# Attention probabilities turned on VectorE and through device memory instead of on TensorE

## The chip, the cores and the metric

The kernel runs on one core of a Trainium2 chip. The metric is the device time of one execution in microseconds (us). A core has TensorE (PE, matrix products into PSUM banks), VectorE (DVE), ScalarE (ACT), GpSimd (POOL) and SyncE (SP). SyncE and GpSimd here mostly start transfers (DMAs), which 16 DMA engines carry out. Each engine runs its own instructions in program order and waits on semaphores for the others.

## The reference, cut to what matters

One decoder layer on 512 tokens of width 2048, in float32: a norm, an attention mixer with 16 heads of width 128 in 4 groups (4 heads share keys and values), an output projection with a residual, a norm, a SwiGLU feed-forward block of width 5632, a residual, and a last norm. With 512 tokens the "selected" branch selects every block and the window covers every token, so a head has three causal branches:

```python
q, kc, vc, ks, vs, kw, vw, gl = jnp.split(h @ w_in, bounds, axis=-1)
gates = jax.nn.sigmoid(gl)                       # three gates for each head and token
kcc, vcc = compress(kc, ...), compress(vc, ...)  # 31 compressed keys and values
p_c = masked_softmax(q @ kcc.T + bias_c, mask_c);  o_c = p_c @ vcc
p_s = masked_softmax(q @ ks.T + bias, causal);     o_s = p_s @ vs
p_w = masked_softmax(q @ kw.T + bias, causal);     o_w = p_w @ vw
out = (g0 * o_c + g1 * o_s + g2 * o_w) @ w_out
```

(This is a summary of the reference's functions in its own names.)

## The kernel before, in words

Every matrix operand is split into a high and a low part (type float32r), and each product is three TensorE products: high x high, high x low, low x high (`three`, lines 265 to 267). A split is a ScalarE copy that rounds to the high part, and a VectorE subtraction that leaves the low part (`split_from`, lines 290 and 291; for weights lines 95 and 96).

The order on every engine is written out by hand: instructions run on each engine in the order in which the program issues them. Weights come as a list of granules of up to 128 x 1024 elements. `granules` writes the list; `Weights.load` issues a granule's DMA on SyncE into one of 3 raw buffers; `Weights.split` splits it into one of 4 converted buffers; `take` hands out the next one and keeps splits and loads some granules ahead.

The attention stage stands between 205 and 722 us of the profile. It mixes two streams. One is attention, head after head. The other is `dense()`, a generator of projection products: queries for a pair of heads (`qpair`), keys and values of the next group (`kpair`, `vpair`), and at the end a part of the output projection (`partial`). `pump(h, step)` runs the dense stream forward until its count of work has reached a goal that grows by one twelfth of a head's share with each step. `drain_to(n)` runs it until n units are done. So TensorE gets dense work between the small attention pieces, and other engines get time for theirs.

A head's queries are cut into four tiles of 128 tokens. Tile t sees the keys of tiles 0 to t, 128(t+1) of them, in each of two full branches, and 31 compressed keys.

- `scores(h, t)`: TensorE writes the scores of all three branches into the PSUM tile `s` (three banks, one copy). For each branch VectorE adds the bias from `TB[h]` (or `biasc`), writes the negated sum into `P[t]` (or `CX[t]` for the compressed branch) and takes its minimum (line 773); ScalarE takes the exponential in place and its sum (line 775).
- `finish(h, t)`: VectorE inverts the sums, multiplies by the gates (lines 780 and 781), and multiplies the three branches by these factors (line 787). The compressed branch is written three times side by side, which makes 96 columns.
- `turn(h, b, kt)`: values need the probabilities with keys on partitions. For key tile kt of branch b, TensorE transposes one 128 x 128 block for each query tile t from kt to 3 into the PSUM tile `pt` (line 797, two buffers). ScalarE and VectorE split it into `pth` and `ptl` (lines 290 and 291; 799 and 800 for the compressed branch).
- `values(h, b, kt)`: TensorE adds the product with the values to the PSUM tile `o` (one bank, one copy).
- `head_out(h)`: `o` is split, and stored to device memory in `d_o` for the first 12 heads (line 824), or kept for the last 4.

The nine pieces (b, kt) of a head are turned one after another, key tile 3 first, and the values of a piece follow two pieces after its turn. The scores of tiles 3 and 2 of the next head stand in the last two steps of a head, those of tiles 1 and 0 at the start of their own head. `load_bias(h + 1)` loads the next head's bias rows into the one buffer `TB` at the start of a head (line 747).

SyncE issues the weight loads (line 79), the bias rows and the stores of `d_o`. GpSimd issues nothing between the stage's first bias row at 197 us and 803 us.

Of the kernel before, what the change touches and what calls it, by code (L numbers as in the profile page):

```python
# [10 lines left out]
F32 = mybir.dt.float32  # L11
# [27 lines left out]
TP_GAP, HN_GAP = 40, 48  # L39
RESYNC = 14  # L40
SPREAD, N_WARM = UL, 24


# [128 lines left out]
def nsa_block(ctx: ExitStack, tc: tile.TileContext, x, rel_bias, mix_g, ffn_g, fin_g, w_in, w_out,  # L172
              pos_k, w1k, w2k, pos_v, w1v, w2v, f_in, f_out, onehot, out):
    nc = tc.nc
# [131 lines left out]
    vcc = keep.tile([96, G, 128], F32R, name="vcc")  # L306
    KK, VV, Q = {}, {}, {}

    def kv_tiles(p, i):
        KK[i] = tuple(p.tile([128, 32 + 2 * S], F32R, name=f"k{i}{n}") for n in "hl")  # L310
        VV[i] = tuple(p.tile([128, NT, 256], F32R, name=f"v{i}{n}") for n in "hl")

    kv_tiles(keep, 0)

# [313 lines left out]
    with ExitStack() as st2:  # L628
        ap_ = st2.enter_context(tc.tile_pool(name="ap", bufs=2))
        ps2 = st2.enter_context(tc.tile_pool(name="ps2", bufs=2, space=PSUM))  # L630
        kv_tiles(ap_, 1)
        P = [ap_.tile([128, 96 + 256 * (t + 1)], F32, name=f"p{t}", bufs=1) for t in range(NT)]
        CX = [ap_.tile([128, 32], F32, name=f"cx{t}", bufs=1) for t in range(NT)]
        for t in range(NT):
            pool.memset(P[t][:, :96], 0.0)
        done = {"n": 0, "ns": 0}

        def stage_tile():
# [95 lines left out]
        def drain_to(n):  # L734
            while done["n"] < n:
# [2 lines left out]
                    return  # L738
                done["ns"] += c or 0

        TB, HS = {}, {}
        sc = ps2.tile([128, 3, 512], F32, name="s", bufs=1).rearrange("p a c -> p (a c)")

# [6 lines left out]
        def offs(t):  # L750
            n = 128 * (t + 1)
            return n, (96, 96 + n)

        def scores(h, t):
            g, (n, off) = h // HPG, offs(t)
# [11 lines left out]
            regions = [(CX[t][:, :NCMP], sc[:, at:at + NCMP], biasc[:, h, 24 - 8 * t:24 - 8 * t + NCMP])]  # L767
            bt = TB[h][:, S - n:].rearrange("p (n s) -> p n s", s=128)
            sw = sc[:, at + 32:at + 32 + 2 * n].rearrange("p (n b s) -> p b n s", b=2, s=128)
            for b in range(2):  # L770
                regions.append((P[t][:, off[b]:off[b] + n].rearrange("p (n s) -> p n s", s=128), sw[:, b], bt))
            for i, (p, ps, bias) in enumerate(regions):
                dve.tensor_tensor_reduce(out=p, in0=ps, in1=bias, op0=OP.add, op1=OP.min, scale=-1.0,
                                         scalar=1e38, accum_out=s["mx"][:, t, i:i + 1])
                act(p, p, AF.Exp, bias=s["mx"][:, t, i:i + 1], scale=-1.0, accum_out=s["sm"][:, t, i:i + 1])
            s[t] = [p for p, _, _ in regions]

        def finish(h, t):
            r = HS[h]["sm"][:, t]
# [2 lines left out]
            for i, p in enumerate(HS[h].pop(t)):  # L782
                o = p
                if not i:
                    o = P[t][:, :96].rearrange("p (n c) -> p n c", n=3)[:, :, :NCMP]
                    p = p.unsqueeze(1).to_broadcast([128, 3, NCMP])
                dve.tensor_scalar(o, p, r[:, i:i + 1], None, op0=OP.mult)

        def turn(h, b, kt):
            pt = ps2.tile([128, 512], F32, name="pt")  # L790
            n = S - 128 * kt
            th = ap_.tile([128, 512], F32R, name="pth")
            tl = ap_.tile([128, 512], F32R, name="ptl")
            rows = slice(0, 128) if b >= 0 else slice(0, 96)
            for t in range(kt, NT):
                src = P[t][:, :96] if b < 0 else P[t][:, offs(t)[1][b] + 128 * kt:][:, :128]
                nc.tensor.transpose(pt[rows, 128 * (t - kt):128 * (t - kt + 1)], src, ident)  # L797
            if b < 0:
                act(th[rows], pt[rows], AF.Copy)
                dve.tensor_tensor(th[32:64], pt[32:64], th[32:64].bitcast(F32), op=OP.subtract)  # L800
            else:
                split_from(pt[:, :n], th[:, :n], tl[:, :n])
            HS[h]["t", b, kt] = th[rows, :n], tl[rows, :n]

        def values(h, b, kt):
            s, g = HS[h], h // HPG
# [20 lines left out]
            del HS[h]  # L827

        load_bias(0)
        pump(-1, 9.7)  # L830
        scores(0, 3)
        pump(-1, 10.5)
        scores(0, 2)
        finish(0, 3)
        pump(-1, 11.2)
        for h in range(H):
            scores(h, 1)
            finish(h, 2)
            pump(h, 0)
            turn(h, 0, 3)  # L840
            scores(h, 0)
            finish(h, 1)
            load_bias(h + 1)
            pump(h, 1)
            turn(h, 1, 3)
            finish(h, 0)
            pump(h, 2)
            seq = [(b, kt) for kt in (3, 2, 1, 0) for b in (0, 1)] + [(-1, 0)]
            for i in range(2, 9):
                turn(h, *seq[i])  # L850
                values(h, *seq[i - 2])
                pump(h, i + 1)
            if h < 13:
                drain_to(h + 1)
            for i in range(2):
# [599 lines left out]
```

## Time and profile before

| what | before |
|---|---|
| median of 3 runs (lowest, highest) | 2156.56 us (2156.32, 2158.26) |
| the profiled execution's own time | 2156.0 us |
| its span | 2154.3 us |
| granted TensorE clock, mean | 0.999 |
| TensorE, VectorE, ScalarE, GpSimd busy | 99%, 73%, 43%, 2% |
| DMA packets, bytes | 242664, 344.02 MB |

The span is the time from the first to the last instruction in the profile. "Busy" is the share of the span in which an engine executes; for TensorE the instructions overlap in a pipeline, so what one costs is read from the distance of starts, or from the chain. The chain is the list of what had to end for the next to begin, followed back from the last instruction. A row of a group gives the line, engine and operation, what is written from what, the shape and count; then the total busy us and the mean ns of one, and after the second bar the idle time before them and what ended it. A row of waits says who waited for whom, and the total us, how often, and the longest.

### The profile page before, as it was taken

To read this page: it belongs to the slowest core of one execution; us is meant where nothing else is said; L and a number is where in the kernel's file an instruction comes from. 1 tells how busy PE (TensorE), PEld (TensorE's weight loads), DVE (VectorE), ACT (ScalarE), POOL (GpSimd) and SP (SyncE) were. 2 spreads that over 40 slices of the span, in tenths; PEclk is the share of its full clock that TensorE was granted. 3 is DMA by queue.
4 is the path that set the end of the run, shared out by engine and by line. 5 is a ranking of instruction groups with operands and counts; after the bars stand their busy time and mean duration, and the time that the engine had idled before them with its cause. 6 is when DMAs were issued, how large, how long until landed. Compare 5 with 4: busy or idle time off the path is not lost.

```text
span 2154.3 us, 37083 instructions
## 1 busy us (share of the span) xinstructions
PE 2137.4 (99%) x15081; PEld 1984.3 (92%) x15081; DVE 1580.8 (73%) x2616; ACT 928.1 (43%) x1433; POOL 53.5 (2%) x108
## 2 busy tenths in 40 slices
PE   9999999999999999999999999999999999999998
PEld 7898898988989888899999999999999888989996
DVE  5565666666665346898888888888888687878785
ACT  5344444444454224343444444343443444444354
POOL 1000000000000000000000000000000000001000
PEclk9999999999999999999999999999999999999999
DMA  7554322332352643343434433334433676878884
GB/s 230 177 153 138 91 94 80 93 96 76 98 213 96 223 139 105 111 144 121 128 118 128 128 128 117 130 117 128 137 120 126 245 283 213 292 275 307 311 328 152
DMA packets 242664, 344.02 MB, mean 160 GB/s; under 512 B 13259, under 2 KB 179195, under 8 KB 241852
## 3 DMA queue, kind: packets, MB, share of 16 engines
q1 hardware_dynamic: 228268, 272.36, 39.2%
q0 software_dynamic: 12320, 65.08, 7.8%
q10 hardware_dynamic: 1904, 4.20, 0.5%
q8 instruction: 118, 1.93, 0.4%
q14 instruction: 54, 0.44, 0.1%
HBM read 298.50 MB, written 48.34 MB: 161 GB/s over the span
## 4 chain that ended last, share of the span: by engine, by line
PE 96%; DVE 2%; ACT 1%; DMA 1%; issue 0%; SPq 0%; ACTq 0%; DVEq 0%
PE f L267 19%; PE f L266 19%; PE f L265 19%; PE proj L265 9%; PE proj L267 9%; PE proj L266 8%; PE pt L797 2%; PE pp L267 1%; PE pp L266 1%; PE pp L265 1%; PE o L266 1%; PE o L267 1%; PE s L265 1%; PE o L265 1%; PE s L267 1%; PE s L266 1%
## 5 line engine op out<-in xcount | busy, mean ns | idle before, releaser
L96 DVE TENSOR_TENSOR wlo<-raw,whi 128x1024 fp32r<-128x1024 f32 (+1 forms) x226 | 272.5, 1208 | 127.6 <-ACT whi L95 126.4
L95 ACT ACTIVATE whi<-raw 128x1024 fp32r<-128x1024 f32 (+1 forms) x226 | 234.7, 1041 | 225.8 <-DVE raw L954 122.5
L954 DVE TENSOR_TENSOR tlo<-tt,thi 128x1536 fp32r<-128x1536 f32 (+2 forms) x135 | 197.1, 1460 | 109.7 <-ACT thi L1056 88.7
L265 PE MATMUL f<-hn_h,whi 128*128 128x256 f32 x984 | 271.7, 276 | 0.8 <-ACT E L1014 0.8
L266 PE MATMUL f<-hn_l,whi 128*128 128x256 f32 x984 | 271.6, 276 | 0.0
L267 PE MATMUL f<-hn_h,wlo 128*128 128x256 f32 x984 | 271.6, 276 | 0.0
L1051 ACT ACTIVATE whi<-raw 128x1024 fp32r<-128x1024 f32 x123 | 126.0, 1057 | 292.2 <-DVE raw L954 282.0
L265 PE MATMUL proj<-hn_h,whi 128*128 128x512 f32 x512 | 204.6, 400 | 0.4 <-ACT hn_h L400 0.4
L267 PE MATMUL proj<-hn_h,wlo 128*128 128x512 f32 x512 | 200.9, 392 | 0.0
L266 PE MATMUL proj<-hn_l,whi 128*128 128x512 f32 x512 | 200.0, 391 | 0.3 <-DVE hn_l L401 0.3
L265 PEld LDWEIGHTS f<-hn_h,whi 128*128 128x128 f32 x984 | 184.7, 188 | 1.2 <-ACT E L1014 1.2
L266 PEld LDWEIGHTS f<-hn_l,whi 128*128 128x128 f32 x984 | 184.7, 188 | 0.0
L267 PEld LDWEIGHTS f<-hn_h,wlo 128*128 128x128 f32 x984 | 184.7, 188 | 0.0
L1056 ACT ACTIVATE thi<-tt 128x1536 fp32r<-128x1536 f32 x82 | 121.9, 1487 | 84.2 <-PE f L266 84.2
L954 DVE TENSOR_TENSOR wlo<-raw,whi 128x1024 fp32r<-128x1024 f32 x123 | 147.0, 1223 | 0.0
L265 PE MATMUL proj<-whi,hn_h 128*128 128x256 f32 (+2 forms) x496 | 146.4, 295 | 0.0
L267 PE MATMUL proj<-whi,hn_l 128*128 128x256 f32 (+2 forms) x496 | 145.4, 293 | 0.0
L266 PE MATMUL proj<-wlo,hn_h 128*128 128x256 f32 (+2 forms) x496 | 145.1, 293 | 0.0
L291 DVE TENSOR_TENSOR ptl<-pt,pth 128x128 fp32r<-128x128 f32 (+3 forms) x128 | 62.4, 488 | 89.4 <-ACT pth L290 89.3
L267 PE MATMUL f<-whi,tlo 128*128 128x512 f32 x320 | 124.9, 390 | 0.6 <-DVE tlo L954 0.6
L266 PE MATMUL f<-wlo,thi 128*128 128x512 f32 x320 | 125.0, 391 | 0.0
L265 PE MATMUL f<-whi,thi 128*128 128x512 f32 x320 | 124.7, 390 | 0.0
(322 smaller groups left out, 6113.1 us busy)
## 6 DMA issues: line engine op xcount, KB each, us to landing
raw<-in_ffn_w_in SPq DMA_DIRECT2D x135, 512.0 KB, 3.5
raw<-in_ffn_w_out SPq DMA_DIRECT2D x88, 512.0 KB, 5.7
raw<-in_nsa_w_in SPq DMA_DIRECT2D x48, 512.0 KB, 3.6
rawx<-in_ffn_w_in SPq DMA_DIRECT2D x41, 512.0 KB, 4.7
raw<-in_nsa_w_out SPq DMA_DIRECT2D x32, 512.0 KB, 3.8
rawx<-d_a SPq DMA_DIRECT2D x31, 512.0 KB, 5.1
raw<-in_nsa_w_in SPq DMA_DIRECT2D x56, 256.0 KB, 3.4
ah<-d_s POOLq DMA_DIRECT2D x16, 896.0 KB, 7.1
```

The source lines that it names most:

```text
L95: self.nc.scalar.activation(hi[:, :n], src, AF.Copy)
L96: self.nc.vector.tensor_tensor(lo[:, :n], src, hi[:, :n].bitcast(F32), op=OP.subtract)
L265: mm(o, ah, bh, start=start, stop=False, skip_group_check=True)
L266: mm(o, ah, bl, start=False, stop=False, skip_group_check=True)
L267: mm(o, al, bh, start=False, stop=stop, skip_group_check=True)
L291: dve.tensor_tensor(lo, psum_ap, hi.bitcast(F32), op=OP.subtract)
L797: nc.tensor.transpose(pt[rows, 128 * (t - kt):128 * (t - kt + 1)], src, ident)
L954: dve.tensor_tensor(o, a, b, op=OP.subtract)
L1051: act(h, r, AF.Copy)
L1056: act(h, ttf, AF.Copy)
```

## The change

`turn` no longer uses TensorE. After `finish` has scaled a tile's probabilities, VectorE transposes the whole tile in place in blocks of 32 x 32. For this `P[t]` is laid out as 4 x runs[t] elements a partition, with runs = 96, 160, 224 and 288: each full branch's keys are split by their 32-wide block within the key tile (index j), and the compressed branch's three copies stand in the last 32 columns of the first three j. The score reduction writes into a new tile `u` (two buffers), and the exponential reads it in the permuted order and writes `P[t]`.

After the block transpose, partition 32 i + a of the tile holds key a of a block, for the queries of block i. Four DMAs issued by GpSimd, one for each 32 partitions, write the tile to device memory as `d_p[t]` in the order (j, a, i, r); a DMA on SyncE (`fetch(t)`) reads it back into `PT` with (j, a), the key, on partitions. A piece is then a view of `PT` (`arrived`), and `turn` is just the split of that view into `pth` and `ptl`, which get three buffers each instead of two.

Tiles 0 and 2 share one buffer, as do tiles 1 and 3. The PSUM tile `pt` is gone. The second group's key and value tiles lose a spare buffer (`bufs=1`).

The order within a head becomes 12 steps. In step i below 9 piece i is turned; in steps 2 to 10 the values of piece i - 2 are multiplied. The next head's scores of tiles 3, 2, 1, 0 stand in steps 5, 7, 9, 11; its finishes of tiles 3, 2, 1 in steps 6, 8, 10, and of tile 0 in step 0 of its own head. The fetches of tiles 3 and 2 stand in steps 9 and 10, those of tiles 1 and 0 in steps 0 and 2. Because scores come half a head sooner, the dense stream makes a group's first query pair before the values instead of after, and `needed(h)` says which units must be done.

```diff
-            out += two(C_KS + c, C_KW + c)
+            out += two(C_KS + c, C_KW + c) + cols(512 * (g + 1))
             off.update((len(out) + i, 32) for i in range(4))
-            out += two(C_VS + c, C_VW + c) + cols(512 * (g + 1))
+            out += two(C_VS + c, C_VW + c)
...
-        P = [ap_.tile([128, 96 + 256 * (t + 1)], F32, name=f"p{t}", bufs=1) for t in range(NT)]
+        runs = [32 * (2 * t + 3) for t in range(NT)]
+        two = [ap_.tile([128, 4 * runs[t]], F32, name=f"p{t}", bufs=1) for t in (2, 3)]
+        P = [two[t % 2][:, :4 * runs[t]].rearrange("p (j r) -> p j r", j=4) for t in range(NT)]
...
+        PT = ap_.tile([128, 4, PT_STEP * 3 + runs[3]], F32, name="ptr", bufs=1)
+        d_p = [dram.tile([4, 32, 4, runs[t]], F32, name=f"d_p{t}") for t in range(NT)]
...
                     yield from kpair(g + 1)
+                    yield from qpair(4 * g + 4)
                     yield from vpair(g + 1)
-                    yield from qpair(4 * g + 4)
...
             for b in range(2):
-                regions.append((P[t][:, off[b]:off[b] + n].rearrange("p (n s) -> p n s", s=128), sw[:, b], bt))
-            for i, (p, ps, bias) in enumerate(regions):
-                dve.tensor_tensor_reduce(out=p, in0=ps, in1=bias, op0=OP.add, op1=OP.min, scale=-1.0,
+                u = ap_.tile([128, S], F32, name="u")[:, :n]
+                regions.append((u.rearrange("p (n s) -> p n s", s=128), u.rearrange("p (n j s) -> p j n s", j=4, s=32),
+                                branch(t, b).rearrange("p j (n s) -> p j n s", s=32), sw[:, b], bt))
+            for i, (u, v, p, ps, bias) in enumerate(regions):
+                dve.tensor_tensor_reduce(out=u, in0=ps, in1=bias, op0=OP.add, op1=OP.min, scale=-1.0,
                                          scalar=1e38, accum_out=s["mx"][:, t, i:i + 1])
-                act(p, p, AF.Exp, bias=s["mx"][:, t, i:i + 1], scale=-1.0, accum_out=s["sm"][:, t, i:i + 1])
+                act(p, v, AF.Exp, bias=s["mx"][:, t, i:i + 1], scale=-1.0, accum_out=s["sm"][:, t, i:i + 1])
...
                 dve.tensor_scalar(o, p, r[:, i:i + 1], None, op0=OP.mult)
+            dve.transpose(P[t], P[t])
+            for i in range(4):
+                pool.dma_start(d_p[t][:, :, i].rearrange("j a r -> a j r"), P[t][32 * i:32 * (i + 1)])
+
+        def fetch(t):
+
+            nc.sync.dma_start(PT[:, :, PT_STEP * t:PT_STEP * t + runs[t]], d_p[t].rearrange("j a i r -> (j a) i r"))
...
         def turn(h, b, kt):
-            pt = ps2.tile([128, 512], F32, name="pt")
...
-            for t in range(kt, NT):
-                src = P[t][:, :96] if b < 0 else P[t][:, offs(t)[1][b] + 128 * kt:][:, :128]
-                nc.tensor.transpose(pt[rows, 128 * (t - kt):128 * (t - kt + 1)], src, ident)
...
+            act(th4, src, AF.Copy)
+            if b < 0:
+                dve.tensor_tensor(th4[32:64], src[32:64], th4[32:64].bitcast(F32), op=OP.subtract)
+            else:
+                dve.tensor_tensor(tl4, src, th4.bitcast(F32), op=OP.subtract)
...
+            for i in range(STEPS):
+                if i == 0:
+                    finish(h, 0)
+                    load_bias(h + 1)
+                    fetch(1)
+                if i == 2:
+                    fetch(0)
+                if i < 9:
+                    turn(h, *seq[i])
                 if h + 1 < H:
-                    scores(h + 1, 3 - i)
-                    if i:
-                        finish(h + 1, 3)
-                values(h, *seq[7 + i])
-                if i:
-                    head_out(h)
-                pump(h, 10 + i)
+                    if i == 5:
+                        drain_to(needed(h + 1))
+                    if i in (5, 7, 9, 11):
+                        scores(h + 1, 3 - (i - 5) // 2)
+                    if i in (6, 8, 10):
+                        finish(h + 1, 3 - (i - 6) // 2)
+                    if i in (9, 10):
+                        fetch(12 - i)
+                if 2 <= i < 11:
...
+                    values(h, *seq[i - 2])
+                    if i == 10:
+                        head_out(h)
+                pump(h, i)
```

More of the change, by code (lines that the diff above doesn't have):

```diff
@@ L40 @@
 RESYNC = 14
+PT_STEP = 224
 SPREAD, N_WARM = UL, 24
@@ L307, in nsa_block, with kv_tiles @@
     KK, VV, Q = {}, {}, {}
-    def kv_tiles(p, i):
-        KK[i] = tuple(p.tile([128, 32 + 2 * S], F32R, name=f"k{i}{n}") for n in "hl")
-        VV[i] = tuple(p.tile([128, NT, 256], F32R, name=f"v{i}{n}") for n in "hl")
+    def kv_tiles(p, i, **kw):
+        KK[i] = tuple(p.tile([128, 32 + 2 * S], F32R, name=f"k{i}{n}", **kw) for n in "hl")
+        VV[i] = tuple(p.tile([128, NT, 256], F32R, name=f"v{i}{n}", **kw) for n in "hl")
     kv_tiles(keep, 0)
@@ L739, in drain_to, with needed @@
                 done["ns"] += c or 0
+        def needed(h):
+            return 4 * ((h - 2) // 4) + (1 if h % 4 > 1 else 3) if h > 1 else 0
         TB, HS = {}, {}
@@ L748, in load_bias, with branch @@
                                                  ap=[[H * UL - 1, 128], [1, S]]))
[L750 to L752 removed]
+        def branch(t, b):
+            return P[t][:, :, 32 * (t + 1) * b:32 * (t + 1) * (b + 1)]
         def scores(h, t):
[L755 removed]
+            g, n = h // HPG, 128 * (t + 1)
             (qh, ql), (kh, kl) = Q[h], KK[g % 2]
@@ L766, in scores @@
                 three(sc[:, at + c0:at + c1], qh[:, tok(t)], ql[:, tok(t)], kh[:, c0:c1], kl[:, c0:c1], True, True)
-            regions = [(CX[t][:, :NCMP], sc[:, at:at + NCMP], biasc[:, h, 24 - 8 * t:24 - 8 * t + NCMP])]
+            c = CX[t][:, :NCMP]
+            regions = [(c, c, c, sc[:, at:at + NCMP], biasc[:, h, 24 - 8 * t:24 - 8 * t + NCMP])]
             bt = TB[h][:, S - n:].rearrange("p (n s) -> p n s", s=128)
@@ L789, in turn, with arrived @@
+        def fetch(t):
+            nc.sync.dma_start(PT[:, :, PT_STEP * t:PT_STEP * t + runs[t]], d_p[t].rearrange("j a i r -> (j a) i r"))
+        def arrived(rows, c0, t0, step):
+            v = PT[:rows, :, c0:c0 + 32]
+            p, i, c = v.ap
+            return bass.AP(tensor=v.tensor, offset=v.offset, ap=[p, [step, NT - t0], i, c])
         def turn(h, b, kt):
-            pt = ps2.tile([128, 512], F32, name="pt")
             n = S - 128 * kt
-            th = ap_.tile([128, 512], F32R, name="pth")
@@ L793, in turn @@
-            tl = ap_.tile([128, 512], F32R, name="ptl")
-            rows = slice(0, 128) if b >= 0 else slice(0, 96)
-            for t in range(kt, NT):
-                src = P[t][:, :96] if b < 0 else P[t][:, offs(t)[1][b] + 128 * kt:][:, :128]
-                nc.tensor.transpose(pt[rows, 128 * (t - kt):128 * (t - kt + 1)], src, ident)
+            th = ap_.tile([128, 512], F32R, name="pth", bufs=3)
+            tl = ap_.tile([128, 512], F32R, name="ptl", bufs=3)
+            rows = 128 if b >= 0 else 96
@@ L798, in turn @@
             if b < 0:
-                act(th[rows], pt[rows], AF.Copy)
-                dve.tensor_tensor(th[32:64], pt[32:64], th[32:64].bitcast(F32), op=OP.subtract)
-            else:
-                split_from(pt[:, :n], th[:, :n], tl[:, :n])
-            HS[h]["t", b, kt] = th[rows, :n], tl[rows, :n]
+                src = arrived(rows, 64, 0, PT_STEP + 64)
+            else:
+                src = arrived(rows, PT_STEP * kt + 32 * (kt + 1) * b + 32 * kt, kt, PT_STEP + 32 * b)
+            th4, tl4 = (x[:rows, :n].rearrange("p (t i s) -> p t i s", i=4, s=32) for x in (th, tl))
@@ L805, in values @@
+            act(th4, src, AF.Copy)
[3 more added lines that the diff above has]
+                dve.tensor_tensor(tl4, src, th4.bitcast(F32), op=OP.subtract)
+            HS[h]["t", b, kt] = th[:rows, :n], tl[:rows, :n]
         def values(h, b, kt):
@@ L829, in nsa_block @@
         load_bias(0)
[L830 to L835, printed above, removed]
-        for h in range(H):
[L837 to L847, printed above, removed]
-            seq = [(b, kt) for kt in (3, 2, 1, 0) for b in (0, 1)] + [(-1, 0)]
[L849 to L855, printed above, removed]
-                if h + 1 < H:
-                    scores(h + 1, 3 - i)
-                    if i:
-                        finish(h + 1, 3)
-                values(h, *seq[7 + i])
-                if i:
-                    head_out(h)
-                pump(h, 10 + i)
+        for i in range(4):
+            scores(0, 3 - i)
+            if i:
+                finish(0, 4 - i)
+            if i > 1:
+                fetch(5 - i)
+            pump(-1, 9 + i)
+        for h in range(H):
+            seq = [(b, kt) for kt in (3, 2, 1, 0) for b in (0, 1)] + [(-1, 0)]
+            for i in range(STEPS):
[7 more added lines that the diff above has]
+                    turn(h, *seq[i])
+                if h + 1 < H:
+                    if i == 5:
[7 more added lines that the diff above has]
+                if 2 <= i < 11:
+                    if i == 2 and h % HPG == 0:
+                        drain_to(h)
+                    values(h, *seq[i - 2])
+                    if i == 10:
+                        head_out(h)
+                pump(h, i)
         drain_to(100)
```

12 lines of the change are left out of this document (7 added, 5 removed).

## The prediction

> **What bounds the kernel now.** I read the page first, then the stage table, then the waits and the chain of the attention stage.
>
> ```profile
> span 2154.3 us, 37083 instructions
> ...
> PE 2137.4 (99%) x15081; PEld 1984.3 (92%) x15081; DVE 1580.8 (73%) x2616; ACT 928.1 (43%) x1433; POOL 53.5 (2%) x108
> ...
> PE 96%; DVE 2%; ACT 1%; DMA 1%; issue 0%; SPq 0%; ACTq 0%; DVEq 0%
> PE f L267 19%; PE f L266 19%; PE f L265 19%; PE proj L265 9%; PE proj L267 9%; PE proj L266 8%; PE pt L797 2%; PE pp L267 1%; PE pp L266 1%; PE pp L265 1%; PE o L266 1%; PE o L267 1%; PE s L265 1%; PE o L265 1%; PE s L267 1%; PE s L266 1%
> ```
>
> TensorE is busy 99% of the span, and the chain that ended last is TensorE for 96%. The lines that the change removes, "PE pt L797", are in that chain with 2%.
>
> The stage table (TensorE, weight load, VectorE, ScalarE, GpSimd; then clock, DMA share, GB/s) shows the attention stage, and two of its heads:
>
> ```profile
> 464.50:497.00 32.50, 32.50 (x171) 27.42 (x170) 20.84 (x63) 15.52 (x41) 0.00 (x0) 1.00 0.32 90
> 205.00:722.00 517.00, 514.38 (x3230) 459.34 (x3229) 324.10 (x984) 245.64 (x644) 0.00 (x0) 1.00 0.33 104
> ```
>
> VectorE works 20.84 us of a head's 32.50, ScalarE 15.52, GpSimd nothing. TensorE's waits from 193 to 760 us are two rows (total, times, longest), 2.5 us in all; none is for a weight, a turned probability or a DMA:
>
> ```profile
> PE s L265 <- DVE mx L773: 2.0, 3, 1.4
> PE pt L797 <- DVE ptl L291: 0.5, 1, 0.5
> ```
>
> So here a microsecond taken from TensorE's stream is a microsecond of the result, as long as the others keep up.
>
> **What goes: the TensorE transposes.** The tile view of pt and three pieces of the chain (start, length):
>
> ```profile
> L797 PE MATMUL pt<-ident,p x384: 270/272/327, 212.8 to 717.0; 128*128 128x128 f32 x160, 128*96 128x128 f32 x32
> ```
> ```profile
> 423.90 0.44 PE pt L797 x4
> 426.99 0.44 PE pt L797 x4
> ...
> 456.42 0.44 PE pt L797 x4
> ```
>
> There are 384, 24 in each of 16 heads. An instruction shows 272 ns, but they overlap: four take 0.44 us of the chain, 0.11 each. 384 x 0.11 = **42.2 us**, 2.64 a head. The same place of the next head follows after 456.42 - 423.90 = 32.52 us, so a head falls to 29.88 and one of its 12 steps to 2.49 us. [...]
>
> **What is added on VectorE.** Each (head, tile) gets one transpose of 384, 640, 896 or 1152 elements a partition, 3072 a head. The trace has no such instruction. The nearest rows:
>
> ```profile
> L291 DVE TENSOR_TENSOR ptl<-pt,pth 128x512 fp32r<-128x512 f32 x32 | 22.0, 688 | 22.4 <-ACT pth L290 22.4
> L787 DVE TENSOR_SCALAR p<-p,sm 128x512 f32<-128x512 f32 x32 | 13.9, 477 | 0.0
> L291 DVE TENSOR_TENSOR ptl<-pt,pth 128x128 fp32r<-128x128 f32 x32 | 9.1, 283 | 0.1
> L787 DVE TENSOR_SCALAR p<-p,sm 128x128 f32<-128x128 f32 x32 | 7.5, 277 | 0.0
> ```
>
> The subtraction costs (688-283)/384 = 1.055 ns an element and 0.148 us fixed; the multiply (477-277)/384 = 0.52 ns and 0.21 us. Low end, like the multiply: 4 x 0.21 + 3072 x 0.00052 = 2.4 us a head. Middle, like the subtraction: 4 x 0.148 + 3.24 = 3.8. High end, two passes of it: 7.1. I take 3.8, the row that moves every element once at full width. [...]
>
> VectorE then has 20.84 + 3.8 = 24.7 of 29.88 us. Not all the rest is free. In one head (423 to 456 us) its idle rows include:
>
> ```profile
> DVE ptl L291 <- ACT pth L290: 5.4, 4, 2.5
> DVE wlo L96 <- ACT whi L95: 1.8, 4, 0.5
> DVE v0l L324 <- ACT v0h L323: 1.1, 2, 0.5
> ```
>
> The first is paced by TensorE and goes, since the turned data now come from memory. The other two, 2.9 us, stay: 27.6 of 29.88, so VectorE fits. It is lumpy, though: steps 5 to 10 hold three of four score reductions, three of four finishes and 1.36 + 1.09 + 0.82 = 3.3 us of the transposes. If by the count of calls 60 to 70 in 100 of the 20.84 fall there, it is 15.8 to 17.9 us in 14.9: VectorE falls 1 to 3 us behind and catches up in steps 11 to 4. TensorE reads a turned piece two steps (5.0 us) after the turn and reuses the score banks two steps later, which hides that. For what leaks (score banks, projection banks at a unit's end) I take 0.3 us a head, **5 us**; bounds 0, and 2.0 a head, 32.
>
> ScalarE copies the turned piece from SBUF instead of PSUM, and writes its exponentials in 32-wide runs; the element counts stay. Rows of a copy from each:
>
> ```profile
> L290 ACT ACTIVATE pth<-pt 128x512 fp32r<-128x512 f32 x32 | 18.9, 592 | 31.8 <-PE o L267 31.8
> ...
> L290 ACT ACTIVATE qh<-yt 128x512 fp32r<-128x512 f32 x14 | 8.9, 633 | 23.5 <-DVE yt L317 23.5
> ```
>
> 41 ns more for each of 9 copies is 0.4 us a head, costed at nothing: ScalarE is free for half of each head. Without that cover it would be 6 us in all.
>
> **The round trip.** Four writes issued by GpSimd, one fetch by SyncE, per (head, tile). Nearest rows (GpSimd's issue, then KB and us from issue to landing):
>
> ```profile
> L487 POOL DMA_DIRECT2D biasc<-d_c x8 | 4.5, 570 | 1.9 <-DMA d_c<-tab 1.9
> ```
> ```profile
> raw<-in_nsa_w_in SPq DMA_DIRECT2D x48, 512.0 KB, 3.6
> ...
> d_s<-al POOLq DMA_DIRECT2D x8, 896.0 KB, 7.9
> ...
> d_o<-of SPq DMA_DIRECT2D x24, 256.0 KB, 2.0
> ...
> tb<-d_u SPq DMA_DIRECT2D x15, 256.0 KB, 3.5
> ...
> hn_l<-d_o SPq DMA_DIRECT2D x3, 1024.0 KB, 10.0
> ...
> d_c<-tab POOLq DMA_DIRECT2D x1, 62.0 KB, 2.1
> ```
>
> Issue 4 x 0.57 = 2.3 us; a write of 48 to 144 KB lands in 2.1 (high end 7.9); a fetch of 192 to 576 KB in 3.6 (high end 10.0). With about 1.6 us of finish and 1.4 of transpose, the trip is 11.0 us; high end 23.2. I take 11.0, because the small pieces are nearest to the 62 and 512 KB rows. The order gives it six steps from finish to turn, 14.9 us, and two more until TensorE reads: 19.9. Covered, with 9 us to spare.
>
> Three queues feel it. ScalarE: tiles 3 and 1 (and 2 and 0) now share one buffer, so the exponential of tile 1 waits until tile 3's four writes have read it, 1.6 + 1.4 + 2.3 + 2.1 = 7.4 us after a finish that stands three steps (7.5 us) ahead; the scores come first, so it just fits. Behind it are the weight splits and the turns. SyncE: fetches of tiles 2, 1 and 0 come two steps (5.0 us) after their finish, so SyncE stands about 2.4 us at each, and the weight loads, the d_o stores and the next bias row queue behind. The loads run several granules ahead, and the bias row, 3.5 us, has five steps. GpSimd has nothing else to do in the stage. The DMA engines:
>
> ```profile
> q1 hardware_dynamic: 56271, 52.95, 32.2%
> ```
>
> 32.2% of 16 engines over 517 us is 47 ns a packet. 4096 more runs a head, 65536, make 194 us of all 16, and the share about 76%: busy, not full.
>
> **The start.** Head 0 has no half head of lead. Before:
>
> ```profile
> 210.64 0.16 DVE L781 TENSOR_TENSOR sm<-sm,gates 128x3 f32<-128x3 f32 x1
> ```
> ```profile
> L265 PEld LDWEIGHTS o<-pth,v0h x64: 187/190/190, 218.6 to 596.2; 128*128 128x128 f32 x64
> ```
>
> From a finish at 210.6 the trip's 11.0 us and a turn (about 0.6) end at 222.2, where TensorE would want the piece near 217: **5 us**, bounds 0 and 10 (later tiles queue behind).
>
> **Sum** against the profiled execution's own 2156.0 us (span 2154.3; the median of the runs is 2156.56, 0.03% above): 2156.0 - 42.2 + 5 + 5 = **2124**. The weight granules' order (queries before values) moves no work, and their due points leave the same lead.
>
> **Rivals.**
> VectorE leads. At the transpose's high end it needs 20.84 + 7.1 + 2.9 = 30.8 us in 29.88, 0.9 a head; with the leak at 2.0 instead: 2156 - 42.2 + 5 + 16 x (0.9 to 2.0) = 2133 to 2151. For: 73% already, and the lump. Against: it is idle a third of a head. 0.14, around 2145.
> Nothing moves: the leak and the start add up to about 42, for instance 2.3 us a head. 2156, 0.04.
> The trip comes late, the one that ends slower. Place: ScalarE at the exponential of tile 1 and at the turn. With writes at 7.9 and fetches at 10.0, the exponential is held 13.2 - 7.5 = 5.7 us and the trip is 23.2; 28.9 against 19.9 stops TensorE 9 us a head: 2156 - 42 + 5 + 144 = 2263. It decides from a trip with hold of 19.9 + 2.64 = 22.5 us. For: 76% DMA share, and the rows at 7.9 and 10.0 us are real landings. Against: those are transfers of 896 and 1024 KB, and the smaller ones land in 2 to 4 us. 0.18, mostly 2165 to 2230. [...]
>
> **Numbers.** Forecast 0.64: with the bounds above, 2113 to 2138 us. About 0.2% (4.3 us) is what a measurement of this kernel can tell from no change. Faster: the forecast and nearly all of the first rival, 0.76. Same 0.05. Slower 0.19. For 8 in 10 I reach from 2111 (nothing leaks, and the 2.5 us of waits go too) to 2165.
>
> **What would show it.** After: no pt instruction on TensorE, heads 29.9 us apart, the stage some 32 to 42 us shorter; 64 transposes on VectorE of about 0.55 to 1.4 us; 256 GpSimd issues near 0.57 us; writes landing near 2.1 and fetches near 3.6. TensorE's waits should stay small except once at the first head. I am wrong if TensorE waits for turned pieces in every head, if ScalarE's long waits are on the writes, or if the transposes cost over 2 ns an element.

## The result, and the profile after

The change made the kernel slower: 2208.09 us (2206.40 to 2209.19) against 2157.41 us (2156.32 to 2158.44) for the kernel before on the same chip, a ratio of 1.0234 [1.0217, 1.0252]. The forecast was 2124 us, and its range ended at 2165.

From the page of the changed kernel, the span, the engines and the chain by engine:

```profile
span 2206.1 us, 37276 instructions
...
PE 2128.4 (96%) x14697; PEld 1964.1 (89%) x14697; DVE 1638.2 (74%) x2680; ACT 927.7 (42%) x1433; POOL 194.4 (9%) x366
...
PE 78%; DVE 10%; ACT 5%; DMA 4%; issue 2%; SPq 0%; ACTq 0%; DVEq 0%
```

TensorE has lost the 384 transposes (15081 to 14697 instructions), and it has lost the chain: 96% before, 78% now. The rest is VectorE, ScalarE and transfers, and it stands in the attention stage. The tile view of `o` times the heads, by the last product of each (the compressed piece); the first row is of the kernel before, the second of the one after:

```profile
L813 PE MATMUL o<-pth,vcc x16: 392/393/398, 242.4 to 722.0; 96*128 96x512 f32 x16
```
```profile
L840 PE MATMUL o<-pth,vcc x16: 393/500/502, 250.1 to 771.1; 96*128 96x512 f32 x16
```

Head 0 ends 7.7 us later. The fifteen periods after it went from (722.0 - 242.4)/15 = 31.97 us to (771.1 - 250.1)/15 = 34.73 us, +2.76 us where the forecast had -2.64 + 0.3. Together 7.7 + 15 x 2.76 = 49.1 us, nearly all of the span's 51.8.

TensorE's waits in the stage, 2.5 us before, are 62 us now; the longest rows (total, times, longest):

```profile
PE proj L266 <- DVE yt L318: 19.5, 10, 2.3
PE proj L266 <- DVE v1l L325: 11.4, 4, 4.9
PE o L267 <- DVE ptl L829: 8.3, 9, 2.2
PE s L266 <- DVE mx L787: 5.6, 10, 1.2
PE proj L266 <- DVE v0l L325: 5.2, 2, 4.9
```

Of them 53 us are for VectorE, and 36 us in three rows are for projection banks that VectorE has not emptied when a projection unit ends (yt, v1l, v0l). Yet VectorE is not full: 74% of the span. Why it is late is read from the chain of one head (start, length; the shortest pieces are not shown):

```profile
444.91 0.19 DVE cx L787
445.11 0.38 DVE u L787
445.49 0.15 issue
445.75 0.74 ACT p L789 x2
446.49 0.60 issue
447.19 0.62 ACT pth L825
447.83 0.69 DVE ptl L829
448.64 0.17 DVE sm L795
448.85 1.08 DVE p L801 x3
450.02 1.24 issue
451.26 1.18 DVE wlo L97
...
455.50 0.96 ACT whi L96
456.48 1.23 DVE wlo L97
...
470.61 0.26 DVE ptl L829
470.92 0.33 PE o L267
```

From the first reduction of the next head's scores (444.91) the chain goes back and forth between VectorE and ScalarE: reductions, exponentials, copy of a turned piece, its subtraction, finish, transpose (the 1.24 us of issue lie inside the block transpose of tile 3, which runs from 449.95 for 1.38), weight splits. TensorE has no part in it until the next head's first turned piece, ready at 470.87, which it takes at 470.92. That is 26.0 us. The two window rows are the whole stage and this stretch (TensorE, weight load, VectorE, ScalarE, GpSimd; clock, DMA share, GB/s):

```profile
205.00:772.00 567.00, 505.66 (x2842) 438.96 (x2841) 380.73 (x1047) 245.73 (x645) 139.57 (x256) 0.95 0.61 183
444.90:470.60 25.70, 22.78 (x146) 20.37 (x144) 19.84 (x58) 12.78 (x35) 6.55 (x12) 1.00 0.53 154
```

In the stretch VectorE is busy 77% and ScalarE 50%: neither is full, but in this chain each step stands in order behind the other engine's answer or behind work of its own. From the score at step 5 to the first values of the next head, at its step 2, TensorE has nine steps of other work, 9 x 2.49 = 22.4 us.

This is one head, and the trip has no part in it. The chain of the whole stage, 205 to 772 us, also holds 74 us of transfers: 9.1% of it are writes of `d_p` and 4.0% fetches. Two of the longest pieces (start, length):

```profile
328.09 5.25 DMA d_p<-p
...
743.88 6.32 DMA d_p<-p
```

The loss to be explained is larger than 51 us. TensorE has 42 us less to do, so it is 51 + 42 = 93 us. On TensorE's side 60 us of them are the added waits, and an estimated 28 us are a lower granted clock in the stage (0.95 instead of 1.00 over 567 us); which engine causes both is what the experiments ask.

### The profile page after: what moved, and what is told of

It reads as the page before. It is cut to its first block, busy times and chain, and to the rows that moved or that the text cites. A ratio compares the mean times of both kernels' runs of the same rounds, so it can differ in the third digit from the quotient of the medians.

```text
span 2206.1 us, 37276 instructions
## 1 busy us (share of the span) xinstructions
PE 2128.4 (96%) x14697; PEld 1964.1 (89%) x14697; DVE 1638.2 (74%) x2680; ACT 927.7 (42%) x1433; POOL 194.4 (9%) x366
## 4 chain that ended last, share of the span: by engine, by line
PE 78%; DVE 10%; ACT 5%; DMA 4%; issue 2%; SPq 0%; ACTq 0%; DVEq 0%
PE f L267 18%; PE f L268 18%; PE f L266 18%; PE proj L266 5%; PE proj L267 5%; PE proj L268 5%; ACT p L789 2%; DMA d_p<-p 2%; DVE p L801 2%; DVE wlo L97 2%; DVE p L802 1%; DVE ptl L829 1%; DMA ptr<-d_p 1%; DVE u L787 1%; PE pp L267 1%
## 5 line engine op out<-in xcount | busy, mean ns | idle before, releaser
L266 PE MATMUL proj<-hn_h,whi 128*128 128x512 f32 x512 | 210.1, 410 | 28.5 <-DVE yt L318 11.5
L267 PE MATMUL proj<-hn_l,whi 128*128 128x512 f32 x512 | 204.7, 400 | 0.3 <-DVE hn_l L402 0.3
L804 POOL DMA_DIRECT2D d_p<-p x256 | 139.6, 552 | 416.9 <-issue 316.5
L266 PEld LDWEIGHTS proj<-hn_h,whi 128*128 128x128 f32 x512 | 99.5, 194 | 51.2 <-DVE yt L318 14.1
```

Source lines behind the costliest of these rows:

```text
L266: mm(o, ah, bh, start=start, stop=False, skip_group_check=True)
L267: mm(o, ah, bl, start=False, stop=False, skip_group_check=True)
L804: pool.dma_start(d_p[t][:, :, i].rearrange("j a r -> a j r"), P[t][32 * i:32 * (i + 1)])
```

## The experiments

All ratios are against the kernel before, run beside each experiment. Where no kernel is named, the edit is made to the changed kernel. The diffs are cut to their main lines. The expectations keep the names that the theories had when they were written: first A, VectorE's lump of work in steps 5 to 10, against B, the trip through device memory. C, D, E and F came later, as the earlier ones fell.

### Which added part costs the time

**Without the block transposes.**

```diff
-            dve.transpose(P[t], P[t])
```

> The changed kernel without the 64 VectorE transposes (so the values are computed from unturned blocks); writes, fetches and order stay. Theory A: VectorE is about 2.5 us less behind in step 8, so the 1.9 us waits for yt nearly go and the 4.9 us waits for v1l and v0l halve: 2155 to 2175 us. Theory B: the trip is 1.4 us shorter at most, 2190 to 2200 us. Theory C (VectorE's total work is the bound): 63 us less work, 2145 us.

Measured: 2157.78 us, 1.0007 [0.9996, 1.0017]. This is in theory A's range; B and C miss. The 3.9 us a head of transposes are worth 50 us. But TensorE still has 42 us less to do than in the kernel before, and the time is no shorter, so some 44 us are lost without the transposes too: TensorE waits 30 us, and the stage's mean clock is 0.98. ScalarE's wait for fetches, below, is longer than with the transposes (67.5 us); what a late trip costs by itself this run does not show:

```profile
ACT pth L824 <- DMA ptr<-d_p: 78.2, 33, 5.2
```

**Without the trip** (no writes and no fetches; the turned pieces are read from a cleared buffer).

```diff
-            for i in range(4):
-                pool.dma_start(d_p[t][:, :, i].rearrange("j a r -> a j r"), P[t][32 * i:32 * (i + 1)])
...
-            nc.sync.dma_start(PT[:, :, PT_STEP * t:PT_STEP * t + runs[t]], d_p[t].rearrange("j a i r -> (j a) i r"))
```

> The changed kernel without the 256 writes and 64 fetches; the turns read a buffer that was cleared once (so the values are zero for attention). Transposes and order stay. Theory A: the waits at the ends of units stay at 1.9 and 4.9 us; only the waits for turned pieces (7 us in the first head, 7 in the last ones, 0.6 in others) and their half clock go: 2180 to 2195 us. Theory B: TensorE runs through, below 2150 us.

Measured: 2188.45 us, 1.0149 [1.0129, 1.0169]. This is in A's range. The trip is worth 20 us of the 93, the transposes 50.

**The order alone**: the twelve steps with TensorE's transposes, two copies of `P`, no block transposes and no transfers.

```diff
-            dve.transpose(P[t], P[t])
...
+                nc.tensor.transpose(pt[rows, 128 * (t - kt):128 * (t - kt + 1)], src, ident)
```

> The new order (scores half a head sooner, 12 steps, units as changed) with the TensorE transposes of the kernel before, two sets of probability buffers, and neither VectorE transposes nor transfers. Theory A: without the 63 us of transposes VectorE reaches the evacuation in time, so the order alone costs little: 2152 to 2165 us, as before. If the order itself is what costs: 2185 us or more, with waits for yt at step 8.

Measured: 2165.52 us, 1.0044 [1.0029, 1.0059]; the order costs 9 us by itself, just outside A's range. The three numbers add up to 50 + 20 + 9 = 79 of the 93 us. No run leaves out transposes and trip together, so how far the two hide each other is not shown.

### Where TensorE feels it

**Units' ends at step 2 instead of step 8.**

```diff
-        def pump(h, step):
-            at = h + (step + 4) / STEPS
-            goal = 20800 * min(at, 13) + 18300 * max(at - 13, 0)
+        def pump(h, step, lead=10):
+            at = h + (step + lead) / STEPS
+            goal = 20800 * min(at, 13) + 16640 * max(at - 13, 0)
```

> The changed kernel with the dense stream led by 10 twelfths of a head instead of 4 (4 still in the lines before head 0), so that a projection unit ends in step 2 and not in step 8; everything else as changed. Theory A (late evacuation: in step 8 the unit's results wait on VectorE behind the finish and transpose of tile 2, TensorE stands for its projection banks, and its clock is halved for some us after): the waits of TensorE for yt, v1l and v0l, 38.7 us together, and most of the half clock, go; about 2140 to 2160 us. Theory B (late trip: turned data come late to ScalarE, and everything stands behind them): the step in which a unit ends does not matter; 2190 us or more.

Measured: 2186.81 us, 1.0138 [1.0121, 1.0155], between the theories. The waits for projection banks went, and others came; TensorE's longest row is now

```profile
PE o L267 <- DVE ptl L829: 24.7, 20, 2.4
```

**A second pair of projection banks**, in the two PSUM banks that the TensorE transposes left free.

```diff
-            return [psx.tile([128, 512], F32, name="proj") for _ in range(2)]
+            pool_ = (psx, ps2)[next(units) % 2]
+            return [pool_.tile([128, 512], F32, name="proj") for _ in range(2)]
```

> Projection units take turns in two pairs of PSUM banks (the two banks that the TensorE transposes used are free), so a unit need not wait until VectorE has emptied the unit before; VectorE's work is the same and in the same order. Theory A (VectorE is about 5 us behind at step 8, and the projection banks are where TensorE feels it; each wait then halves the granted clock for some us): the 36 us of waits of proj for yt, v1l and v0l go, most of the clock loss with them: 2145 to 2170 us, and what is left are waits for turned pieces and mx. Theory B (VectorE is late altogether, the waits only move, as in the run with the unit ends at step 2): waits of o for ptl and pth grow to 25 us or more, 2180 to 2205.

Measured: 2208.15 us, 1.0234 [1.0218, 1.0249]: nothing. A miss for A, and above B's range. No wait for a projection bank is left, and the time stands elsewhere, above all at the score banks:

```profile
PE s L266 <- DVE mx L790: 33.9, 17, 3.1
PE o L267 <- DVE ptl L832: 10.9, 8, 2.1
```

**Two multiplies of each finish moved to ScalarE**, alone and with the second banks.

```diff
-                dve.tensor_scalar(o, p, r[:, i:i + 1], None, op0=OP.mult)
+                if i:
+                    act(o, p, AF.Copy, scale=r[:, i:i + 1])
+                else:
+                    dve.tensor_scalar(o, p, r[:, i:i + 1], None, op0=OP.mult)
```

> The two branch multiplies of each finish (128 a head-tile pair, 2560 elements a partition and head) move from VectorE to ScalarE, which is half idle; VectorE loses about 2.9 us a head, nearly what the transposes added (3.9). Theory A (VectorE's lump in steps 5 to 10): most of the lag goes, 2165 to 2185 us. Theory B (ScalarE and the trip behind it set the end): ScalarE, which stands in writes' waits, becomes later still, 2205 to 2230.

> Both together. Theory A: 2125 to 2150 us, below both kernels, with the start (about 7 us) and a few us of turned pieces left. Theory B: 2180 or more.

Measured: 2222.26 us, 1.0304 [1.0289, 1.0319], and 2223.58 us, 1.0305 [1.0288, 1.0323]. VectorE lost some 2.9 us a head of its 3.9 us more (busy 377.4 us between 205 and 760 us in the changed kernel, 331.9 in the first run), and the kernel became 14 us slower. Both runs miss A and lie in B's ranges. So VectorE's load by itself does not set the time: the multiplies stay in the same chain, on the other engine, and each tile's transpose now waits for them:

```profile
DVE p L805 <- ACT p L802: 61.2, 64, 6.0
```

**TensorE's waits filled with idle work.** In the changed kernel TensorE's granted clock was 1.00 from 485 to 495 us and 0.51 from 500 to 505; the rows are before, at and after a wait of 4.9 us that ended at 499.5:

```profile
485.00:495.00 10.00, 9.23 (x56) 7.40 (x54) 7.56 (x19) 4.02 (x10) 2.18 (x4) 1.00 0.50 141
495.00:500.00 5.00, 0.49 (x1) 0.49 (x2) 3.16 (x13) 2.80 (x9) 2.19 (x4) 0.80 0.84 230
500.00:505.00 5.00, 5.00 (x15) 4.00 (x15) 2.95 (x13) 1.57 (x8) 2.18 (x4) 0.51 0.50 117
```

Are the 28 us of clock a cost of their own?

```diff
+            if 0 < next(units) < 14:
+                f = ps2.tile([128, 512], F32, name="fill", bufs=1)
+                for i in range(8):
+                    mm(f, hn_h[:, 15, :128], hn_h[:, 15], start=True, stop=True, skip_group_check=True)
```

> The changed kernel with 8 extra matrix products of 128x512 (about 1.7 us) into a spare bank ahead of each projection unit of the stage after the first, 13 x 1.7 = 22 us of work for TensorE that serves nothing but to fill its waits there. Theory A (a wait of about 2 us or more costs its own time and then a stretch at half clock): the filled waits cost the same, the half clock goes, 2183 to 2200 us though 22 us of work were added. Theory B (the low clock is no consequence of the waits): 2208 if the extra work fits the waits, up to 2230 if it does not, the clock still near 0.95.

Measured: 2206.36 us, 1.0226 [1.0211, 1.0242]. With an estimated 24 us more work (104 products; 128x512 products start 0.23 us apart in the trace of the kernel before, and the expectation had 22), a clock of 0.97 instead of 0.95 and waits for yt of 5.9 instead of 19.5 us, the time is the same: above A's range, and B had 2208 with the clock still near 0.95. The run does not decide. TensorE's waits fell by 12 us in all and some 11 us of clock came back (0.02 of 555 us), together about what the fill added. That fits another engine setting the time, with the low clock as a consequence, but also a clock that costs and a fill that ate its gain.

### What holds VectorE

**Scores sooner.** The chain of 26 us against nine steps gave theory C: more steps, less wait.

```diff
-                    if i in (5, 7, 9, 11):
-                        scores(h + 1, 3 - (i - 5) // 2)
...
+                    j = i + 2
...
+                    if j in (5, 7, 9, 11):
+                        scores(h + 1, 3 - (j - 5) // 2)
```

The finishes and the next bias row move with the scores, and the fetch of tile 0 comes a step sooner.

> The changed kernel with the scores of the next head two steps sooner (steps 3, 5, 7, 9 instead of 5, 7, 9, 11) and each finish with them; fetches, turns and values stay (the fetch of tile 0 a step sooner), the work is the same. Theory C, new: from the first score of a head to its last turned piece VectorE and ScalarE answer each other in one serial chain (reduction, exponential, copy of a piece, subtraction, finish, transpose), 25.7 us in the head from 444.9 to 470.6, where the order gives TensorE only nine steps, 22.4 us, of other work; where it waits, and at which clock it idles, is a consequence. Two steps more, 27.4 us, cover the chain: TensorE leads again, 2125 to 2150 us. Theory D (VectorE's and ScalarE's work of a head simply does not fit, or the buffers shared by tiles 3 and 1 and the trip bind): nothing gained, 2195 or more.

> The same with one step (scores at 4, 6, 8, 10). Theory C: ten steps are 24.9 us against 25.7, so about 0.8 us a head are left of 3.3: 2150 to 2175 us. Theory D: 2195 or more.

> Two steps sooner, and the projection units take turns in two pairs of banks. Theory C: no more than a few us below the run with two steps sooner alone, 2122 to 2145. If the projection banks do bind once TensorE leads again: 10 to 30 us below it.

Measured: two sooner 2211.38 us, 1.0259 [1.0233, 1.0285]; one sooner 2208.17 us, 1.0236 [1.0218, 1.0255]; two sooner with the second banks 2172.75 us, 1.0073 [1.0057, 1.0088]. Two edits that do nothing each bring 35 us together: banks and lead hide each other. As a forecast C was wrong for all three (for the third it had 2145 as the highest), so 26.0 against 22.4 us alone does not explain the time: with 27.4 us of room and one pair of banks nothing was gained.

**The scores spread evenly**, at steps 0, 3, 6, 9, with and without the second banks; and two sooner with banks and the units' ends at step 2.

```diff
-                    if i in (5, 7, 9, 11):
-                        scores(h + 1, 3 - (i - 5) // 2)
-                    if i in (6, 8, 10):
-                        finish(h + 1, 3 - (i - 6) // 2)
+                    if i in (0, 3, 6, 9):
+                        scores(h + 1, 3 - i // 3)
+                    if i in (1, 4, 7, 10):
+                        finish(h + 1, 3 - i // 3)
```

The even order also loads each bias row two heads ahead into a second buffer, stores `o` through a shared tile, and fetches tile 0 a step sooner; what these bring alone was not tried.

> The next head's scores at steps 0, 3, 6, 9 and its finishes at 1, 4, 7, 10, so that the same work is spread over the head, and projection units in two pairs of banks. Theory C (the lump): 2125 to 2150 us, below both kernels, with VectorE's idle time spread and waits of TensorE under 10 us in the stage, the first head's 5 included. Theory D (too long a chain whatever the order): 2165 or more, like the 2173 of two steps sooner with these banks.

> The same even order with one pair of projection banks. Theory C: 2130 to 2165 us, since VectorE is not behind where a unit ends. Theory D, or if any wait of VectorE behind ScalarE is enough to hold the banks: 2190 to 2212.

> Scores two steps sooner, two pairs of banks, and the units' ends moved from step 8 to step 2, where no score and no finish stands: about 2.7 us of VectorE's work a head leave the lump. Theory C: 2140 to 2160 us. Theory D: 2168 to 2180, as without the move.

Measured: 2185.70 us, 1.0136 [1.0121, 1.0151]; 2184.58 us, 1.0130 [1.0115, 1.0145]; 2169.61 us, 1.0059 [1.0042, 1.0076]. The even order gains 23 us; the first and the third run fell in D's ranges, the second between the two. C misses all three. But D's reason, too much work in series, is not what the trace shows. What VectorE and TensorE wait for in the even order with the banks:

```profile
DVE wlo L97 <- ACT whi L96: 83.0, 58, 2.2
DVE ptl L832 <- ACT pth L828: 27.7, 18, 5.8
```
```profile
PE o L843 <- DVE pth L830: 34.1, 14, 3.3
```

VectorE stands 83 us in front of weight splits: the subtraction is issued right behind ScalarE's copy, so VectorE waits 1.4 us for it 58 times, with a finish and a turned piece queued behind.

**The subtraction a granule later** (three steps), with the even order and banks; then with the units' ends at step 5; then on two sooner, banks, step 2; then alone. Loads run two granules ahead instead of three.

```diff
-        self.nc.vector.tensor_tensor(lo[:, :n], src, hi[:, :n].bitcast(F32), op=OP.subtract)
+        self.late.append(lambda: self.nc.vector.tensor_tensor(lo[:, :n], src, hi[:, :n].bitcast(F32), op=OP.subtract))
+        while len(self.late) > self.lag:
+            self.late.pop(0)()
```

> Even order with two pairs of banks, and in the stage each weight granule's subtraction on VectorE is issued one granule (three steps) after its copy on ScalarE; the loads run two granules ahead instead of three. Theory E (VectorE is not short of time, it stands in order behind ScalarE: 92 us for whi): that wait falls below 20 us and the time from 2186 to 2140-2165. Theory D (too much work in series): 2180 or more, and the wait turns up elsewhere.

> The same, and the projection units end at step 5 instead of step 8, so that the scaling of a finished projection no longer stands ahead of the compressed piece at step 8. Theory E: the 34 us wait of o for pth at line 830 goes too: 2125 to 2150. Theory D: 2175 or more.

> Scores two steps sooner, two pairs of banks, units' ends at step 2, and the late subtraction of the weight splits. VectorE waits 54 us for whi there, 15 us of the loss against the kernel before remain. Theory E: 2145 to 2160. Theory D, or the trip (fetches stand for 14% of the chain in that run): 2165 or more.

> The changed kernel with the weight splits' subtractions a granule later and nothing else. Theory E in its strong form (this stand is what makes VectorE late everywhere): 2165 to 2185. Theory F (several limits in a row, each hiding the next: the lump, the banks, the stand): 2200 to 2212, since in this order VectorE waits only 9.7 us for whi.

Measured: 2145.75 us, 0.9945 [0.9930, 0.9960]; **2144.90 us, 0.9946 [0.9930, 0.9963]**; 2150.44 us, 0.9972 [0.9958, 0.9985]; alone 2198.81 us, 1.0197 [1.0180, 1.0214]. With the same work on every engine the even order went from 2185.70 to 2145.75, so D fell, and the first three runs are in E's ranges. They are 0.3 to 0.6% faster than the kernel before, little but clear of the spread. Alone the edit gives 9 us: E's strong form misses, and F is off by 1 us. VectorE's rows for turned pieces and for whi in the first of the four, and TensorE's waits and the engines of the second:

```profile
DVE ptl L836 <- ACT pth L832: 76.8, 61, 6.0
DVE wlo L98 <- ACT whi L97: 29.1, 6, 12.6
```
```profile
PE o L270 <- DVE ptl L836: 7.3, 17, 1.3
PE o L269 <- ACT pth L832: 6.4, 6, 4.7
PE s L269 <- DVE mx L794: 4.0, 2, 3.3
PE s L269 <- DVE yt L321: 1.7, 1, 1.7
PE o L847 <- DVE pth L834: 0.3, 1, 0.3
```
```profile
PE 2106.3 (98%) x14697; PEld 1946.3 (91%) x14697; DVE 1636.2 (76%) x2680; ACT 925.9 (43%) x1433; POOL 194.4 (9%) x366
```

Up to 700 us, just before the heads end (708.8), no stand for whi is left; the 6 in the row come later. The expectation wanted that wait below 20 us, and part of it turned up elsewhere: VectorE now stands 49 us longer for ScalarE's copies of turned pieces. There it hurts TensorE less. In the even order with the banks TensorE's waits fell from 49 to 26 us with the late subtraction, and its clock rose from 0.96 to 0.99. In the second run they are 19.7 us, where the changed kernel had 62, and VectorE is busy 1636 us, where it was 1638.

## Why the prediction was wrong, point by point

- **TensorE sets the end, so a microsecond off it is a microsecond of the result, as long as the others keep up.** Right for the kernel before; the others did not keep up, and of the 93 us lost some 60 are TensorE's waits and 28 its clock.
- **The 42.2 us of TensorE transposes.** In the best version a head takes
```profile
L847 PE MATMUL o<-pth,vcc x16: 393/498/503, 251.6 to 708.3; 96*128 96x512 f32 x16
```
  (708.3 - 251.6)/15 = 30.45 us, 1.52 less than before. Without the 4.0 and 1.7 us for mx and yt, which fall ahead of head 0's end, 14 us of the waits lie in these fifteen heads; 22.8 + 14 = 37 of the forecast's 15 x 2.64 = 39.6 us can be seen. The saving is there; the changed kernel could not use it.
- **VectorE's transposes at 3.8 us a head.** Right. The four sizes, largest and smallest:
```profile
L802 DVE STREAM_TRANSPOSE p<-p 128x1152 f32<-128x1152 f32 x16 | 22.1, 1379 | 0.6
...
L802 DVE STREAM_TRANSPOSE p<-p 128x384 f32<-128x384 f32 x16 | 9.3, 578 | 0.6
```
  (1379 - 578)/768 = 1.04 ns an element, 62.7 us in all, 3.9 a head: the subtraction's price, as taken.
- **"27.6 of 29.88, so VectorE fits"; behind by 1 to 3 us, hidden, with a leak of 0.3 us a head.** This is the step that failed. The leak is 2.76 + 2.64 = 5.4 us a head, 81 us in fifteen. The test compared a sum of busy and listed waiting time with a period, and gave the hand-written order no cost. The runs showed a cost in its place: transposes of 3.9 us a head that fit by the sum are worth 50 us, 3.1 a head, and the same work on every engine takes 2208 us in one order and 2145 in another with a second pair of banks. One head's chain shows where the sum looks away: 26.0 us of reductions, exponentials, splits, finishes and transposes that stand behind each other on two engines, against 22.4 us of TensorE's work in between. That the length of this chain is the cause is a reading; more room alone gained nothing, and banks, lead and the order of the weight splits each hid another limit. Nor do the waits stay as the old order had them: VectorE's wait for whi was 9.7 us in the changed kernel's stage and 83 in the even order. The forecast also gave TensorE two steps of slack at each place; at a unit's end there was little, as 36 us of waits for projection banks show.
- **The round trip.** Its issues came out as forecast, 0.55 us for 0.57. Its transfers were longer: by size the writes took 2.6 to 4.7 us, forecast at 2.1, and the fetches 3.3 to 5.3, forecast at 3.6. The largest:
```profile
L804 POOL DMA_DIRECT2D d_p<-p x256 | 139.6, 552 | 416.9 <-issue 316.5
...
d_p<-p POOLq DMA_DIRECT2D x64, 144.0 KB, 4.0
ptr<-d_p SPq DMA_DIRECT2D x16, 576.0 KB, 5.3
```
  ScalarE waited 67.5 us for fetches, and 11.1 us for writes at the shared buffers, and VectorE's largest wait is for ScalarE's copies of the fetched pieces:
```profile
ACT pth L825 <- DMA ptr<-d_p: 67.5, 28, 5.9
...
ACT p L789 <- DMA d_p<-p: 11.1, 5, 4.9
```
```profile
DVE ptl L829 <- ACT pth L825: 83.0, 39, 5.2
```
  The DMA share is 0.61 where 0.76 was forecast. Taking the whole trip away gains 20 us, so "covered, with 9 us to spare" failed too, and the sum had no term for it. The rival of the late trip named 2165 to 2230, and 2208 lies in there, but with no trip at all the time is still 2188: the trip is a part of the loss, not most of it.
- **The start at 5 us.** 7.7, within its bounds.
- **The rival "VectorE leads".** The right engine for the wrong reason: it was to need the transposes at 7.1 us. They cost 3.9, and its place was not the sum but the order; its 2133 to 2151 had no term for that.
- **A term that was missing: TensorE's clock after a wait.** By the stage's mean clock, 0.95 instead of 1.00, it is an estimated 28 of the 93 us. Whether it costs by itself or only comes with the waits, the filled waits do not decide.
- **The range.** Its upper end of 2138 does not follow from the bounds named: with 32 us of leak and 10 at the start they reach 2156. The measured 2208 lies outside both.
- **The signs of being wrong.** None of the three came: TensorE's waits for turned pieces were 0 to 0.6 us a head but for the first and the last two, ScalarE's long waits were on fetches rather than writes, and the transposes cost 1.04 ns an element. The place of the loss, projection banks and VectorE's order, was not among them.

What stays open: 2144.9 is still 21 us above the forecast. In that run TensorE's waits make up 19.7 us, the first head's among them; how much of them the trip holds was not tried in that order.

## What to carry to other kernels

Before work is moved from a full engine to one with idle time, lay out the chain that the moved work joins, from what starts it to what the full engine needs, over every engine that answers in between, and compare its length with the work that the order puts beside it; a busy share, 73% of VectorE before, does not show that. When one remedy changes nothing, look where the wait went before dropping it: second banks, scores two steps sooner, units' ends at step 2 and the later subtraction gained 0, -3, 21 and 9 us alone and 58 together. Issue an instruction that needs another engine's answer some steps after the one that it answers, so that nothing queues behind the round trip: that was worth 40 us in the even order and 9 in the changed one.

## What the runs showed of the hardware

In the changed kernel TensorE's granted clock was 0.50 for about 5 us after the wait of 4.9 us that ended at 499.5. A wait of 1.93 us that ended at 320.8 was also followed by a clock of 0.50, from 321 to 323, while after one of 2.26 us that ended at 461.9 it was 1.00, from 462 to 464. Of these two waits near 2 us the shorter one was followed by the lower clock, so their length alone does not decide, and not every wait had a lower clock behind it. In the run with scores two steps sooner, two pairs of banks and the units' ends at step 2, there were 33 waits for mx with 34.8 us in all, none over 2.3, and the stage's mean clock was 1.00.
